# A weight-splitting planner that counts GpSimd and VectorE as excluding each other on SBUF operands

## The chip, the cores and the metric

The kernel runs on one core of a Trainium2 chip. The metric is the device time of one execution in microseconds (us). A core has five engines with a queue each: TensorE (PE in the rows; PEld is its weight load), VectorE (DVE), ScalarE (ACT), GpSimd (POOL) and SyncE (SP), which here issues all DMAs. Each engine takes its instructions strictly in the order in which they were written, and waits on semaphores for the others.

## The reference, cut to what matters

One decoder block over x of 512 x 1024 in float32: an RMS norm, one wide projection, two token mixers (sparse attention with compressed, selected and sliding branches, and chunkwise retention with 4 heads), gates, an output projection and a residual.

```python
h = rms_norm(x, norm_pre)
proj = h @ w_in                                   # 1024 x 6936
o_a = nsa(q_n, k_c, v_c, k_s, v_s, k_w, v_w, g_n) # attention, 8 heads of 64
y_a = (o_a * silu(z_n)) @ w_nsa_o
o_b = retention(rope(q_r), rope(k_r), v_r)        # 4 heads, chunks of 128
y_b = (o_b * silu(z_r)) @ w_ret_o
merged = sigmoid(m_a) * y_a + sigmoid(m_b) * y_b
y = x + rms_norm(merged @ w_out, norm_post)
```

## The kernel before

Every large product is made of three matmuls on operands that were split into a high part (rounded to the matmul's fp32r type) and a low part (the rest): high times high, high times low, low times high. So each half of a loaded weight tile (`raw`, 128 x 1024, two halves of 128 x 512) needs two operations before TensorE can use it: a copy to `whi`, by `cp_any` (L167) on ScalarE or VectorE, and a subtraction `wlo = raw - whi`, by `split_lo` (L373) and `sub_split` on VectorE or GpSimd. There are 168 halves, 8 of them 280 columns wide (they go to `arena_r`), the rest 512. Nine pairs `whi`/`wlo` and three `raw` buffers stand ahead of TensorE.

The order of all instructions is made while the program is built, by a planner (class `Order`). Work is written as coroutines: `main` is the long row of weight matmuls (low priority), and tails (rotary embedding, softmax, retention chunks, gates) are spawned from it with higher priority. `Order` keeps a planned time for TensorE (`now`) and one for each other engine (`eng`); each helper adds its price in ns: `tt` for two-tensor operations (VectorE, or GpSimd with e="pool"), `ts`, `stt`, `cp_any`, `mm` for matmuls. Before TensorE's next piece is written, `Order.run` asks which coroutine could go on by the planned time. A tail's transposes or matmuls are thus written between the main matmuls at the place where the planner thinks their operands ready; if they are late on the chip, TensorE waits there, with the main matmuls queued behind.

The engine of a half is chosen by planned times as well. For `wlo`, with `DVE_BIAS` of 900 in GpSimd's favour:

```python
e = "dve" if max(od.eng["dve"], r) + 1.04 * c < max(od.eng["pool"], r) + 2.25 * c - DVE_BIAS else "pool"
```

In the order of the program the stages are: norm, keys and values (`tail_a`, `tail_c`, with `rope16` at L176 and `doubled` at L523), queries (`tail_q`), compression, attention (`att_head` with L798 and L185, `att_block`), retention (`tail_qk`, `ret`), and the gated outputs. The names in the rows: `bank` is PSUM; `arena_f`, `arena_r`, `nat`, `raw`, `whi`, `wlo` lie in SBUF; L197 are matmuls, L201 transposes.

Of the kernel before, what the change touches and what calls it, by code (L numbers as in the profile page):

```python
# [18 lines left out]
P = 128  # L19
# [10 lines left out]
LAG, PE_LAG = 150.0, 110.0  # L30
MARGIN = 50.0
WAKE = 5, 2
HOOKS = 1, 3, 4, 5
DVE_BIAS = 900


class Order:
# [4 lines left out]
    def __init__(self):  # L42
        self.now = 0.0
        self.eng = {"act": 0.0, "dve": 0.0, "pool": 0.0, "dma": 0.0}
        self.ring = 500.0
        self.cos = []
        self.flags = set()

# [8 lines left out]
        self.now = max(self.now, r + LAG + PE_LAG) + cost  # L57
        return self.now + 47

    def op(self, e, cost, r=0.0):  # L60
        self.eng[e] = max(self.eng[e], r + LAG) + cost
        return self.eng[e]

    def dma(self, nbytes, r=0.0, n=1):
# [49 lines left out]
def block_kernel(ctx: ExitStack, tc, x, norm_pre, w_in, b_gate, pe_k, w1_k, w2_k,  # L114
# [27 lines left out]
    od = Order()  # L142


    def size(a):
        n = 1
        for k in a.shape[1:]:
            n *= k
        return n

    def far(a):
        return a.space == PSUM

    def act_ns(o, i, k=0):
        return 0.833 * size(o) + (51 if far(i) else 93) + 93 * k

    def copy_ns(o, i, k=0):
        return (1.042 if far(i) else 0.521) * size(o) + 69 + 61 * k

    def lazy(*vals):  # L160
        return sum(v is not None and not isinstance(v, (int, float)) for v in vals)

    def act(o, i, func=AF.Copy, r=0.0, **kw):
        S.activation(o, i, func, **kw)  # L164
        return od.op("act", act_ns(o, i, lazy(*kw.values())), r)

    def cp_any(o, i, r=0.0):  # L167

        cd = copy_ns(o, i)
        if max(od.eng["act"], r) + act_ns(o, i) <= max(od.eng["dve"], r) + cd:  # L170
            return act(o, i, r=r)
        V.tensor_copy(o, i)  # L172
        return od.op("dve", cd, r)

    def tt(o, a, b, op, r=0.0, e="dve"):
        (V if e == "dve" else G).tensor_tensor(o, a, b, op=op)  # L176
        if op == OP.pow:
            return od.op(e, 300 + 164 * size(o), r)
        return od.op(e, (1.042 * size(o) + 69) if e == "dve" else (2.25 * size(o) + 73), r)

    def ts(o, a, s1, s2, op0, op1=None, r=0.0):
        if op1 is None:
            V.tensor_scalar(o, a, s1, None, op0=op0)
        else:
            V.tensor_scalar(o, a, s1, s2, op0=op0, op1=op1)  # L185
        return od.op("dve", copy_ns(o, a, lazy(s1, s2)), r)

    def stt(o, a, s, b, op0, op1, r=0.0):
        V.scalar_tensor_tensor(o, a, s, b, op0=op0, op1=op1)  # L189
        return od.op("dve", 1.042 * size(o) + 69 + 61 * lazy(s), r)  # L190

    def recip(o, a, r=0.0):
        V.reciprocal(o, a)
# [1 line left out]

    def mm(ps, a, b, start, stop, r=0.0, cost=None):
        T.matmul(ps, a, b, start=start, stop=stop)  # L197
        return od.pe(cost or max(0.4167 * size(b) + 2.5, 107 if a.shape[-1] > 64 else 54), r)

    def tr(ps, a, idn, r=0.0):  # L200
        T.transpose(ps, a, idn)  # L201
# [2 lines left out]
    def mm3(ps, ah, al, bh, bl, first, last, r=0.0):  # L204
        mm(ps, ah, bh, first, False, r)
        mm(ps, ah, bl, False, False)
        return mm(ps, al, bh, False, last)

    def sub_split(lo, src, hi, r, e="dve"):
        return tt(lo, src, f(hi), OP.subtract, r, e)  # L210
# [124 lines left out]
    def load_next():  # L335
        i = len(raws)
        if i < len(loads):
            raw = rp.tile([P, 1024], FT, name="raw", tag="raw", bufs=NR)
            loads[i][0](raw)
            raws.append((raw, od.dma(P * loads[i][1] * 4, parts[2 * (i - NR) + 1][2] if i >= NR else 0.0, loads[i][2])))  # L340
            for fn in hook.get(i, ()):
                fn()
# [5 lines left out]
    def splitter():  # L348
        for i, (_, n, _, perm) in enumerate(loads):
            for k in range(2):  # L350
                p = 2 * i + k
                own = KD <= p < 2 * KD
                yield lambda: own or in_ring(p) < in_ring(len(done)) + NW
                while len(raws) <= i:
                    load_next()
                r = max(raws[i][1], done[-1] if done and not own else 0.0)
                yield r
                m = n // 2
                src = raws[i][0][:, k * m:(k + 1) * m]
                if own:  # L360
                    hi, lo = WC[p - KD]
                else:
                    hi = wp.tile([P, 512], FR, name="whi", tag="whi", bufs=NW)
                    lo = wp.tile([P, 512], FR, name="wlo", tag="wlo", bufs=NW)
                vh, vl = hi[:, :m], lo[:, :m]
                if perm:
                    src = src.rearrange("p (g j c) -> p g j c", g=2, j=4)
                    vh, vl = (v.rearrange("p (j g c) -> p g j c", g=2, j=4) for v in (vh, vl))
                e = cp_any(vh, src, r)
                od.spawn(split_lo(p, hi, lo, src, vh, vl, e), 0)  # L370
                yield

    def split_lo(p, hi, lo, src, vh, vl, r):  # L373
        yield r
        c = size(vl)
        e = "dve" if max(od.eng["dve"], r) + 1.04 * c < max(od.eng["pool"], r) + 2.25 * c - DVE_BIAS else "pool"
        r = sub_split(vl, src, vh, r, e)
        yield lambda: len(parts) == p
        parts.append((hi, lo, r))
        if p % 2 and len(raws) <= p // 2 + NR:  # L380
            load_next()
# [61 lines left out]
    def norm_tile(t):  # L443
        yield lambda: t in xarr
        xa = xt[t]
        ss = sp.tile([P, 2], FT, name="ss", tag="ss", bufs=4)
        for i, (c, ra) in enumerate(xarr[t]):
            yield ra
            ra = act(junk[:, c], xa[:, c], AF.Square, scale=1.0 / 32.0, accum_out=ss[:, i:i + 1], r=ra)
        yield ra  # L450
        rv = sp.tile([P, 1], FT, name="rv", tag="rv", bufs=4)
        if len(xarr[t]) == 2:
            ra = ts(rv, ss[:, 0:1], ss[:, 1:2], 1e-6, OP.add, OP.add, ra)
        else:
            ra = ts(rv, ss[:, 0:1], 1e-6, None, OP.add, r=ra)
        rs = sp.tile([P, 1], FT, name="rr", tag="rr", bufs=4)
        ra = tt(rs, rv, nhalf[:, 0:1], OP.pow, ra, "pool")
        yield ra
        for half in range(2):
            hc = slice(half * 512, half * 512 + 512)  # L460
            ra = stt(xa[:, hc], xa[:, hc], rs, npre[half], OP.mult, OP.mult, ra)
            od.spawn(norm_half(t, half, ra), 0)
        if t == NT - 1:
            for b in npre:
                PS.put(b, ra)
# [35 lines left out]
    def rope16(v, t, shape, r, e="dve"):  # L501

        n = int(np.prod(shape))
        pat = {1: "p (a c) -> p a c", 2: "p (a b c) -> p a b c"}[len(shape)]
        kw = dict(zip("ab", shape))
        t1, t2 = (at(41 + 0.5 * i, n * 16).rearrange(pat, **kw) for i in range(2))

        def bc(a):
            c = a.shape[-1]
            for _ in shape:  # L510
                a = a.unsqueeze(1)
            return a.broadcast_to([P, *shape, c])
        ix = (slice(None),) * (1 + len(shape))
        lo, hi, al = ix + (slice(0, 8),), ix + (slice(8, 16),), ix + (slice(0, 16),)
        tt(t1, v[al], bc(ropen[:, t, 0:16]), OP.mult, r, e)
        tt(t2[lo], v[hi], bc(ropen[:, t, 16:24]), OP.mult, r, e)
        tt(t2[hi], v[lo], bc(ropen[:, t, 24:32]), OP.mult, r, e)
        return tt(v[al], t1, t2, OP.add, 0.0, e)

    def doubled(kn, a, b, kd, r):  # L520

        n = (b - a) // 64
        V.tensor_copy(kd.rearrange("p (a r c) -> p a r c", a=n, r=2),  # L523
                      kn[:, a:b].rearrange("p (a c) -> p a c", c=64).unsqueeze(2).broadcast_to([P, n, 2, 64]))
        return od.op("dve", 0.6 * n * P + 70, r)

    def keysT(kd, off, br, t, r):
        ps = yield from PT.get()
# [68 lines left out]
    def tail_z(j, ps, e):  # L597
        yield e
        e = act(szn[:, j, :], ps, AF.Tanh, r=e, scale=0.5)
        yield e  # L600
        e = stt(szn[:, j, :], szn[:, j, :], 1.0, ps, OP.add, OP.mult, e)
        ACC.put(ps, e)
        od.flags.add(f"Z{j}")

    def gates():
        yield od.need("C0", "C1", "C2", "C3")
        e = act(gate, gate, AF.Tanh, scale=0.5)
        yield e
        ts(gate, gate, 0.25, 0.25, OP.mult, OP.add, e)
        od.flags.add("gate")  # L610
# [32 lines left out]
    def compress(i, ph, e):  # L643
# [20 lines left out]
        e = act(u, u, AF.Tanh, scale=0.7978845608028654, r=e)  # L664
        yield e
        e = stt(hx, u, 1.0, hx, OP.add, OP.mult, e)
        po = yield from PT.get()
        if i == 0:
# [691 lines left out]
```

## Time and profile before

| | |
|---|---|
| median of 3 runs | 565.32 us (565.24 to 566.01) |
| profiled execution | 565.26 us, of which the span is 563.5 us |
| TensorE busy | 533.2 us, 95% of the span |
| VectorE busy | 395.3 us, 70% |
| ScalarE busy | 227.1 us, 40% |
| GpSimd busy | 204.1 us, 36% |
| DMA | 53.1 MB, mean 94 GB/s |

The span is what the profiler saw of the instructions; 1.8 us of the execution lie around it. Busy times of engines overlap. Matmuls are pipelined, so that a record of 0.39 us stands for one every 0.225 us. Records on VectorE overlap their successor by some 0.08 us as well, so what an operation takes of the engine is the distance of two starts.

### The profile page before, as it was taken

What the parts mean: (1) busy time and instruction counts of PE and PEld (TensorE: products, weight loads), DVE (VectorE), ACT (ScalarE), POOL (GpSimd) and SP (SyncE); (2) the same over time, 40 slices, a digit from 0 to 9 for tenths busy, and PEclk for the clock granted to TensorE, in tenths of its full rate; (3) what the DMA queues carried; (4) which work ended last, traced back from release to release, by engine and by line L of the source; (5) the groups of instructions that cost most, each with busy time, mean ns of one, the idle gap of its engine ahead of it and who ended that gap; (6) DMA issues with size and microseconds to landing.
All of it is one profiled execution on the core that took longest, in us unless ns stands there. A gap on an engine that the chain in (4) does not pass through costs nothing.

```text
span 563.5 us, 7554 instructions
## 1 busy us (share of the span) xinstructions
PE 533.2 (95%) x2668; PEld 440.7 (78%) x2668; DVE 395.3 (70%) x803; ACT 227.1 (40%) x502; POOL 204.1 (36%) x195
## 2 busy tenths in 40 slices
PE   7969998979999989999999999899999999999995
PEld 5748886868888868878787788787888888887885
DVE  5989569998979999877786657755555342637353
ACT  4632456754547755645242435341212221103211
POOL 7643105850240432635215534333422251505220
PEclk9998999989999999999999999999999999999999
DMA  7633003650040130421314331317340440524023
GB/s 260 199 110 102 19 1 112 173 162 4 7 143 1 43 108 24 145 76 42 109 33 136 99 89 41 109 33 242 116 133 22 129 130 22 153 70 148 17 96 113
DMA packets 33672, 53.13 MB, mean 94 GB/s; under 512 B 4065, under 2 KB 14177, under 8 KB 33634
## 3 DMA queue, kind: packets, MB, share of 16 engines
q1 hardware_dynamic: 33634, 52.65, 31.0%
q8 instruction: 21, 0.34, 0.2%
q14 instruction: 17, 0.14, 0.1%
HBM read 50.54 MB, written 2.10 MB: 93 GB/s over the span
## 4 chain that ended last, share of the span: by engine, by line
PE 61%; DVE 27%; issue 5%; DMA 3%; POOL 2%; ACT 2%; DVEq 0%; POOLq 0%; SPq 0%; ACTq 0%
PE bank L197 57%; DVE arena_f L176 5%; DVE arena_r L176 4%; PE bank L201 4%; DVE wlo L176 4%; DVE arena_f L185 3%; DVE whi L172 3%; DMA raw<-in_w_in_dram 3%; DVE arena_f L798 2%; DVE arena_f L189 1%; DVE nat L176 1%; POOL wlo L176 1%; POOL nat L176 1%; ACT arena_r L164 0%; ACT whi L164 0%
## 5 line engine op out<-in xcount | busy, mean ns | idle before, releaser
L176 POOL TENSOR_TENSOR wlo<-raw,whi 128x512 fp32r<-128x512 f32 x103 | 144.3, 1414 | 213.1 <-PE bank L197 92.7
L197 PE MATMUL bank<-whi,hTh 128*128 128x512 f32 x256 | 104.8, 409 | 0.3 <-ACT hTh L164 0.3
L197 PE MATMUL bank<-whi,hTl 128*128 128x512 f32 x256 | 100.8, 394 | 1.0 <-DVE hTl L176 1.0
L197 PE MATMUL bank<-wlo,hTh 128*128 128x512 f32 x256 | 100.6, 393 | 0.7 <-POOL wlo L176 0.7
L164 ACT ACTIVATE whi<-raw 128x512 fp32r<-128x512 f32 x100 | 62.0, 629 | 60.0 <-PE bank L197 41.6
L164 ACT ACTIVATE arena_r<-bank 128x512 fp32r<-128x512 f32 (+2 forms) x88 | 50.0, 573 | 68.0 <-PE bank L201 61.8
L172 DVE CAST whi<-raw 128x512 fp32r<-128x512 f32 x60 | 44.6, 747 | 45.5 <-PE bank L197 38.2
L197 PE MATMUL bank<-arena_r 128*128 128x256 f32 (+2 forms) x328 | 72.9, 341 | 3.5 <-DVE arena_r L176 3.0
L176 DVE TENSOR_TENSOR arena_r<-bank,arena_r 128x512 fp32r<-128x512 f32 (+2 forms) x80 | 52.0, 658 | 27.1 <-ACT arena_r L164 26.5
L176 DVE TENSOR_TENSOR wlo<-raw,whi 128x512 fp32r<-128x512 f32 x57 | 61.3, 1084 | 4.3 <-ACT whi L164 2.5
L197 PE MATMUL bank<-hTh,whi 128*128 128x512 f32 x160 | 63.3, 396 | 0.9 <-DVE whi L172 0.9
L197 PE MATMUL bank<-hTh,wlo 128*128 128x512 f32 x160 | 62.7, 392 | 0.8 <-POOL wlo L176 0.6
L197 PE MATMUL bank<-hTl,whi 128*128 128x512 f32 x160 | 62.4, 390 | 0.0
L197 PEld LDWEIGHTS bank<-arena_r 128*128 128x128 f32 x328 | 51.1, 191 | 11.8 <-DVE arena_r L176 5.5
L197 PE MATMUL bank<-arena_r,whi 128*128 128x512 f32 x192 | 59.1, 389 | 0.0
L197 PEld LDWEIGHTS bank<-whi,hTl 128*128 128x128 f32 x256 | 48.3, 189 | 12.1 <-DVE hTl L176 1.4
L201 PE MATMUL bank<-ident,arena_f 128*128 128x128 f32 (+1 forms) x294 | 45.3, 279 | 11.7 <-DVE arena_f L523 4.8
L197 PEld LDWEIGHTS bank<-wlo,hTh 128*128 128x128 f32 x256 | 48.4, 189 | 9.2 <-POOL wlo L176 1.2
L197 PEld LDWEIGHTS bank<-whi,hTh 128*128 128x128 f32 x256 | 48.3, 189 | 8.6 <-ACT hTh L164 0.5
L201 PEld LDWEIGHTS bank<-ident,arena_f 128*128 128x128 f32 (+1 forms) x294 | 35.1, 141 | 23.9 <-DVE arena_f L176 6.2
L164 ACT ACTIVATE arena_f<-bank 128x512 f32<-128x512 f32 (+2 forms) x42 | 22.3, 530 | 75.8 <-PE bank L197 75.4
L197 PE MATMUL bank<-whi,arena_r 128*128 128x512 f32 (+1 forms) x176 | 49.0, 353 | 0.1
(116 smaller groups left out, 792.2 us busy)
## 6 DMA issues: line engine op xcount, KB each, us to landing
raw<-in_w_in_dram SPq DMA_DIRECT2D x44, 512.0 KB, 3.7
raw<-in_w_in_dram SPq DMA_DIRECT2D x16, 256.0 KB, 3.2
raw<-in_w_ret_o_dram SPq DMA_DIRECT2D x8, 512.0 KB, 4.9
raw<-in_w_out_dram SPq DMA_DIRECT2D x8, 512.0 KB, 3.8
arena_f<-in_x_dram SPq DMA_DIRECT2D x7, 512.0 KB, 5.8
raw<-in_cmp_w_k_dram SPq DMA_DIRECT2D x8, 256.0 KB, 3.7
arena_f<-in_rope_r_dram SPq DMA_DIRECT2D x8, 256.0 KB, 2.7
raw<-in_cmp_w_v_dram SPq DMA_DIRECT2D x8, 256.0 KB, 3.5
```

The source lines that it names most:

```text
L164: S.activation(o, i, func, **kw)
L172: V.tensor_copy(o, i)
L176: (V if e == "dve" else G).tensor_tensor(o, a, b, op=op)
L185: V.tensor_scalar(o, a, s1, s2, op0=op0, op1=op1)
L189: V.scalar_tensor_tensor(o, a, s, b, op0=op0, op1=op1)
L197: T.matmul(ps, a, b, start=start, stop=stop)
L201: T.transpose(ps, a, idn)
L798: V.tensor_tensor_reduce(pv[:, b, :], sv[:, b, :], maskp[:, 512 - L:512], 1.0, -NEG, OP.add, OP.min, nm[:, b:b + 1])
```

## The change

The planner gets a second time, `port`. Operations on VectorE whose operands all lie in SBUF, and all on GpSimd, begin no earlier than `port` and move it to their end; `begin` gives the planned start. `split_lo` compares planned ends with `begin` for both engines, and its bias of 900 in GpSimd's favour is gone; `cp_any` gets a bias of 400 ns in ScalarE's favour. Some prices move: a GpSimd subtraction of 512 columns from 1225 to 1285 ns, a matmul of 512 columns from 216 to 228 ns, and the doubling copy. No arithmetic changes.

```diff
--- before.py
+++ after.py
@@ -31,7 +31,7 @@
 MARGIN = 50.0
 WAKE = 5, 2
 HOOKS = 1, 3, 4, 5
-DVE_BIAS = 900
+DVE_BIAS = 400
 
 
 class Order:
@@ -43,6 +43,7 @@
         self.now = 0.0
         self.eng = {"act": 0.0, "dve": 0.0, "pool": 0.0, "dma": 0.0}
         self.ring = 500.0
+        self.port = 0.0
         self.cos = []
         self.flags = set()
 
@@ -57,8 +58,14 @@
         self.now = max(self.now, r + LAG + PE_LAG) + cost
         return self.now + 47
 
-    def op(self, e, cost, r=0.0):
-        self.eng[e] = max(self.eng[e], r + LAG) + cost
+    def begin(self, e, r=0.0, port=False):
+        return max(self.eng[e], r + LAG, self.port if port else 0.0)
+
+    def op(self, e, cost, r=0.0, port=False):
+
+        self.eng[e] = self.begin(e, r, port) + cost
+        if port:
+            self.port = self.eng[e]
         return self.eng[e]
 
     def dma(self, nbytes, r=0.0, n=1):
@@ -151,6 +158,9 @@
     def far(a):
         return a.space == PSUM
 
+    def near(*aps):
+        return not any(far(a) for a in aps)
+
     def act_ns(o, i, k=0):
         return 0.833 * size(o) + (51 if far(i) else 93) + 93 * k
 
@@ -167,27 +177,27 @@
     def cp_any(o, i, r=0.0):
 
         cd = copy_ns(o, i)
-        if max(od.eng["act"], r) + act_ns(o, i) <= max(od.eng["dve"], r) + cd:
+        if od.begin("act", r) + act_ns(o, i) <= od.begin("dve", r, near(i)) + cd + DVE_BIAS:
             return act(o, i, r=r)
         V.tensor_copy(o, i)
-        return od.op("dve", cd, r)
+        return od.op("dve", cd, r, near(i))
 
     def tt(o, a, b, op, r=0.0, e="dve"):
         (V if e == "dve" else G).tensor_tensor(o, a, b, op=op)
         if op == OP.pow:
-            return od.op(e, 300 + 164 * size(o), r)
-        return od.op(e, (1.042 * size(o) + 69) if e == "dve" else (2.25 * size(o) + 73), r)
+            return od.op(e, 300 + 164 * size(o), r, True)
+        return od.op(e, (1.042 * size(o) + 69) if e == "dve" else (2.36 * size(o) + 77), r, e == "pool" or near(o, a, b))
 
     def ts(o, a, s1, s2, op0, op1=None, r=0.0):
         if op1 is None:
             V.tensor_scalar(o, a, s1, None, op0=op0)
         else:
             V.tensor_scalar(o, a, s1, s2, op0=op0, op1=op1)
-        return od.op("dve", copy_ns(o, a, lazy(s1, s2)), r)
+        return od.op("dve", copy_ns(o, a, lazy(s1, s2)), r, near(o, a))
 
     def stt(o, a, s, b, op0, op1, r=0.0):
         V.scalar_tensor_tensor(o, a, s, b, op0=op0, op1=op1)
-        return od.op("dve", 1.042 * size(o) + 69 + 61 * lazy(s), r)
+        return od.op("dve", 1.042 * size(o) + 69 + 61 * lazy(s), r, near(o, a, b))
 
     def recip(o, a, r=0.0):
         V.reciprocal(o, a)
@@ -195,7 +205,7 @@
 
     def mm(ps, a, b, start, stop, r=0.0, cost=None):
         T.matmul(ps, a, b, start=start, stop=stop)
-        return od.pe(cost or max(0.4167 * size(b) + 2.5, 107 if a.shape[-1] > 64 else 54), r)
+        return od.pe(cost or max(0.4435 * size(b) + 1, 107 if a.shape[-1] > 64 else 54), r)
 
     def tr(ps, a, idn, r=0.0):
         T.transpose(ps, a, idn)
@@ -373,7 +383,7 @@
     def split_lo(p, hi, lo, src, vh, vl, r):
         yield r
         c = size(vl)
-        e = "dve" if max(od.eng["dve"], r) + 1.04 * c < max(od.eng["pool"], r) + 2.25 * c - DVE_BIAS else "pool"
+        e = "dve" if od.begin("dve", r, True) + 1.04 * c < od.begin("pool", r, True) + 2.36 * c else "pool"
         r = sub_split(vl, src, vh, r, e)
         yield lambda: len(parts) == p
         parts.append((hi, lo, r))
@@ -522,7 +532,7 @@
         n = (b - a) // 64
         V.tensor_copy(kd.rearrange("p (a r c) -> p a r c", a=n, r=2),
                       kn[:, a:b].rearrange("p (a c) -> p a c", c=64).unsqueeze(2).broadcast_to([P, n, 2, 64]))
-        return od.op("dve", 0.6 * n * P + 70, r)
+        return od.op("dve", 0.53 * n * P + 70, r, True)
 
     def keysT(kd, off, br, t, r):
         ps = yield from PT.get()
```

All of the order of the program is made anew with this. Over the whole program the `wlo` operations of 512 columns go from 103 on GpSimd and 57 on VectorE to 11 and 149; the `whi` copies of 512 columns go from 100 on ScalarE and 60 on VectorE to 148 and 12; of the 280-column halves, 3 subtractions move from GpSimd to VectorE and 3 copies from VectorE to ScalarE. TensorE has the same matmuls in another interleaving. SyncE has the same DMAs; one load of `raw` stands one place earlier against its neighbours, and one pair later.

First place: VectorE in the stage of keys and values, around the rotary embedding of the third tile (`nat_104`), whose doubled keys (the COPY) are what TensorE transposes next. Before:

```order
L176 TENSOR_TENSOR arena_f<-bank_85,pe_113 64x2x7x16
L176 TENSOR_TENSOR arena_f<-nat_104,ropen 128x64
L176 TENSOR_TENSOR arena_f<-nat_104,ropen 128x4x8 x2
L176 TENSOR_TENSOR nat_104<-arena_f 128x2x2x16
L523 COPY arena_f<-nat_104 128x768
L176 TENSOR_TENSOR arena_f<-bank_86,pe_112 64x2x8x16 x2
L176 TENSOR_TENSOR arena_f<-bank_86,pe_113 64x2x8x16 x2
L176 TENSOR_TENSOR wlo<-raw,whi 128x512
L176 TENSOR_TENSOR arena_r<-bank_85,arena_r 128x2x128
```

After:

```order
L186 TENSOR_TENSOR arena_f<-bank_86,pe_113 64x2x7x16
L186 TENSOR_TENSOR arena_f<-nat_104,ropen 128x64
L186 TENSOR_TENSOR arena_f<-nat_104,ropen 128x4x8 x2
L186 TENSOR_TENSOR nat_104<-arena_f 128x2x2x16
L533 COPY arena_f<-nat_104 128x768
L186 TENSOR_TENSOR wlo<-raw,whi 128x512 x5
L186 TENSOR_TENSOR arena_r<-bank_85,arena_r 128x2x128
L186 TENSOR_TENSOR arena_f<-bank_86,pe_112 64x2x8x16 x2
```

Five subtractions now stand behind the COPY and ahead of the low part of the transposed keys (`arena_r`), which stands some places earlier against the sums with `pe`.

GpSimd at the same place; the operations on `nat` are the low parts of values. Before:

```order
L176 TENSOR_TENSOR arena_r<-nat_103,arena_r 128x64 x2
L176 TENSOR_TENSOR wlo<-raw,whi 128x512
L176 TENSOR_TENSOR arena_r<-nat_104,arena_r 128x64 x2
L176 TENSOR_TENSOR wlo<-raw,whi 128x512 x4
L176 TENSOR_TENSOR arena_r<-nat_102,arena_r 128x64 x2
L176 TENSOR_TENSOR wlo<-raw,whi 128x512
L176 TENSOR_TENSOR gate<-nat_103,bg 128x24
```

After:

```order
L186 TENSOR_TENSOR arena_r<-raw,arena_r 128x280
L186 TENSOR_TENSOR arena_r<-nat_103,arena_r 128x64 x2
L186 TENSOR_TENSOR arena_r<-nat_104,arena_r 128x64 x2
L186 TENSOR_TENSOR arena_r<-nat_102,arena_r 128x64 x2
L186 TENSOR_TENSOR gate<-nat_103,bg 128x24
```

The six subtractions of 512 columns are gone from GpSimd here.

Second place: VectorE at the start of attention, behind the rotary embedding of the queries in `nat_103`; L798 and L185 belong to the softmax of one head, `arena_r<-bank` are low parts that TensorE needs. Before:

```order
L176 TENSOR_TENSOR nat_103<-arena_f 128x8x16
L176 TENSOR_TENSOR arena_r<-bank_85,arena_r 128x512
L798 ISA arena_f,stat<-bank_84,maskp 128x512
L798 ISA stat 128x1
L172 CAST whi<-raw 128x512
L193 RECIPROCAL stat<-stat 128x1
L185 TENSOR_SCALAR arena_f<-arena_f,stat,gate 128x512
L176 TENSOR_TENSOR arena_r<-nat_103,arena_r 128x8x64
L176 TENSOR_TENSOR arena_r<-bank_86,arena_r 128x512
```

After:

```order
L186 TENSOR_TENSOR arena_r<-nat_103,arena_r 128x8x64
L808 ISA arena_f,stat<-bank_84,maskp 128x512
L808 ISA stat 128x1
L186 TENSOR_TENSOR arena_r<-bank_85,arena_r 128x512
L182 CAST whi<-raw 128x512
L203 RECIPROCAL stat<-stat 128x1
L195 TENSOR_SCALAR arena_f<-arena_f,stat,gate 128x512
L186 TENSOR_TENSOR arena_r<-bank_86,arena_r 128x512
L186 TENSOR_TENSOR wlo<-raw,whi 128x512 x3
```

Three subtractions in a row stand on VectorE here now; before, four in a row of this stretch stood on GpSimd.

## Rows read from the trace of the kernel before

**Rows 1.** Windows: length, busy PE, PEld, DVE, ACT, POOL; clock, DMA share, GB/s.

```profile
0.00:60.00 60.00, 49.77 (x258) 39.16 (x259) 48.62 (x99) 25.57 (x61) 31.87 (x56) 0.97 0.51 157
60.00:130.00 70.00, 64.02 (x356) 53.28 (x355) 59.49 (x137) 41.91 (x93) 28.08 (x24) 0.98 0.33 95
130.00:260.00 130.00, 127.42 (x675) 106.12 (x674) 113.27 (x304) 73.23 (x188) 41.16 (x35) 1.00 0.20 59
260.00:400.00 140.00, 134.55 (x671) 111.36 (x670) 91.68 (x165) 52.48 (x97) 53.39 (x45) 1.00 0.32 96
...
400.00:563.50 163.50, 157.45 (x716) 130.81 (x714) 82.29 (x102) 33.95 (x64) 49.61 (x37) 1.00 0.31 97
```

**Rows 2.** Waits of TensorE: us in total, times, longest.

```profile
PE bank L197 <- DVE arena_r L176: 5.2, 6, 2.3
PE bank L201 <- DVE arena_f L523: 4.8, 2, 3.8
...
PE bank L201 <- DVE hTl L176: 1.3, 1, 1.3
```

**Rows 3.** Groups by line and shape: count, busy us, mean ns, idle before.

```profile
L176 POOL TENSOR_TENSOR wlo<-raw,whi 128x512 fp32r<-128x512 f32 x103 | 144.3, 1414 | 213.1 <-PE bank L197 92.7 <-DVE whi L172 44.9 <-ACT whi L164 34.8
...
L164 ACT ACTIVATE whi<-raw 128x512 fp32r<-128x512 f32 x100 | 62.0, 629 | 60.0 <-PE bank L197 41.6 <-DMA raw<-in_w_in_dram 12.4 <-DMA raw<-in_w_out_dram 3.1
L176 DVE TENSOR_TENSOR wlo<-raw,whi 128x512 fp32r<-128x512 f32 x57 | 61.3, 1084 | 4.3 <-ACT whi L164 2.5
...
L172 DVE CAST whi<-raw 128x512 fp32r<-128x512 f32 x60 | 44.6, 747 | 45.5 <-PE bank L197 38.2 <-DMA raw<-in_w_ret_o_dram 2.7 <-DMA raw<-in_w_in_dram 2.1
```

**Rows 4.** Timeline, VectorE where GpSimd is idle: start, us, operation, count.

```profile
14.88 0.69 DVE L176 TENSOR_TENSOR wlo<-raw,whi 128x512 fp32r<-128x512 f32 x1
15.49 0.42 DVE L172 CAST whi<-raw 128x512 fp32r<-128x512 f32 x1
15.83 0.68 DVE L176 TENSOR_TENSOR hTl<-bank,hTh 128x512 fp32r<-128x512 f32 x1
...
23.15 0.23 DVE L176 TENSOR_TENSOR nat<-arena_f 128x64 f32<-128x64 f32 x1
```

**Rows 5.** Timeline at the first place, 36 to 43 us, three engines.

```profile
36.34 4.98 POOL L176 TENSOR_TENSOR wlo<-raw,whi 128x512 fp32r<-128x512 f32 x4 [0.76 <-ACT whi L164]
...
36.95 3.19 DVE L176 TENSOR_TENSOR arena_f<-nat,ropen 128x64 f32<-128x64 f32 x3
40.18 1.22 DVE L176 TENSOR_TENSOR nat<-arena_f 128x64 f32<-128x64 f32 x1
...
42.05 0.44 PE L201 MATMUL bank<-ident,arena_f 128*128 128x128 f32 x2 [3.79 <-DVE arena_f L523]
```

**Rows 6.** Windows of a clock dip and of a dense stretch; columns as in rows 1.

```profile
43.30:46.70 3.40, 3.12 (x10) 2.15 (x9) 3.28 (x6) 0.00 (x0) 0.00 (x0) 0.50 0.12 34
...
450.00:500.00 50.00, 50.00 (x223) 41.39 (x222) 22.80 (x27) 9.23 (x15) 17.07 (x12) 1.00 0.36 106
```

**Rows 7.** Timeline of the second place and the longest wait of that stage.

```profile
86.95 5.84 POOL L176 TENSOR_TENSOR wlo<-raw,whi 128x512 fp32r<-128x512 f32 x4 [22.31 <-DVE stat L193]
...
86.92 1.61 DVE L185 TENSOR_SCALAR arena_f<-arena_f,stat,gate 128x512 f32<-128x512 f32 x1
88.45 1.78 DVE L176 TENSOR_TENSOR arena_r<-nat,arena_r 128x512 fp32r<-128x512 f32 x1
...
94.51 0.55 DVE L185 TENSOR_SCALAR arena_f<-arena_f,stat,gate 128x512 f32<-128x512 f32 x1
...
122.08 1.11 PE L197 MATMUL bank<-arena_f 128*128 128x64 f32 x4 [2.27 <-DVE arena_r L176]
```

**Rows 8.** Timeline in retention, 349 to 355 us.

```profile
349.41 3.00 POOL L176 TENSOR_TENSOR wlo<-raw,whi 128x512 fp32r<-128x512 f32 x2
...
351.18 1.78 DVE L176 TENSOR_TENSOR arena_r<-arena_f,arena_r 128x512 fp32r<-128x512 f32 x1
...
354.14 0.66 PE L201 MATMUL bank<-ident,arena_f 128*128 128x128 f32 x4 [1.15 <-DVE arena_f L176]
```

## Prediction, made before the changed kernel ran

> **What bounds the kernel now.** I read the windows by stage first [rows 1]. Their TensorE busy times add up to 533.2 of 563.5 us, so TensorE sets the end and what can be won is its idle time: 10.2 us from 0 to 60 (60 minus 49.8), 6.0 from 60 to 130, 2.6 from 130 to 260, 5.5 from 260 to 400 and 6.1 in the rest. From 450 to 500 us TensorE has no gap, at 50/222 = 0.225 us a matmul of 512 columns [rows 6]; what is idle behind 400 us is all but wholly the end of the last tail (norm, residual, store), and about 2 us at the beginning are start-up. So some 22 us of the idle time lie where an order can reach it. It is not lack of DMA: its share is 0.20 to 0.32 between 130 and 400 us [rows 1].
>
> The waits of TensorE come next [rows 2]: nearly all name VectorE. The groups and the timeline then say why VectorE is late. Its `wlo` takes 1084 ns in the mean and its copy to `whi` 747 [rows 3], but 0.69 and 0.42 us where GpSimd is idle [rows 4]. At the first place GpSimd runs four `wlo` from 36.34 to 41.32 us, and in that time VectorE spends 3.19 us on three tiny rotary products and 1.22 on a fourth operation [rows 5] that takes 0.23 alone [rows 4]: each waits out one GpSimd subtraction of about 1.25 us. The COPY behind them releases TensorE after 3.79 us idle. The planner before knows nothing of this, so it wrote the transposes where VectorE would have been ready without it. At the second place the same: 1.61 and 1.78 us for operations that take 0.55 and some 0.69 alone, beside four GpSimd subtractions [rows 4, 7]; and in retention 1.78 us instead of 0.69 ahead of a wait of 1.15 [rows 8].
>
> Idle time costs a second time: behind the waits of 3.79 and 2.27 us the granted clock is 0.50 (the level of 1.2 GHz) for 3.4 us, with 3.12 us busy [rows 5 to 7]. That is some 1.5 us of lost matmul time, at two places, of which [rows 6] show the first: 3 us in all.
>
> **The change part by part.**
>
> *92 subtractions of 512 columns go from GpSimd to VectorE, 48 copies from VectorE to ScalarE.* On VectorE a subtraction costs 0.61 us from start to start and a copy 0.34 [rows 4], so 92 x 0.61 - 48 x 0.34 = 56 - 16 = +40 us of work. Against it stands the time in which VectorE no longer waits for GpSimd. From below: the stretch of `wlo` and `whi` alone is 57 x (1.08 - 0.69) + 60 x (0.75 - 0.42) = 22 + 20 = 42 us [rows 3, 4], over 103 GpSimd subtractions 0.41 us each. From above: at the second place the two stretched operations beside four subtractions lost 1.06 + 1.09 = 2.15 us and a third, not in the rows, about as much, so 0.8 each. 92 x 0.41 to 92 x 0.8 is 38 to 74 us. VectorE's load therefore changes by +2 to -34 us of 395. I take -15: the many small operations of the first stage are in neither group of rows 3. VectorE gets little lighter, but its times get to be those that the planner reckons with, and that is the gain.
>
> ScalarE takes 48 x 0.63 = 30 us more [rows 3], on 227 busy; in its fullest stretch (130 to 260 us, 73 of 130) it gets some 6 more. This is covered; without that cover it would be late low parts, one copy of 0.63 each. GpSimd's own tails (rotary differences, low parts of values) no longer queue behind subtractions; I cost that at nothing. One weight load moves a place earlier on SyncE and a pair moves later; they lie tiles ahead in the ring of three `raw` buffers, so nothing, and one landing of some 4 us if that ring ran dry.
>
> *0 to 60 us.* The wait of 3.79 goes: four operations that cost 4.4 us [rows 5] cost about 0.65 without GpSimd's four subtractions, and the five that come to VectorE stand behind the COPY. Behind these five are the low part of the transposed keys and the sums with `pe`: 3.0 us later at worst, with the next transposes waiting for them, but the main matmuls have then been placed by a planner that counts these 3.0 us. The wait of 1.3 on `hTl` [rows 2] has the same rotary operations ahead of it and goes too. Of the 10.2 idle, 2 are start-up and 5.1 these two; of the 3.1 left I take half, and the clock dip of 1.5. Sum 3.8 + 1.3 + 1.5 + 1.5 = 8.1; bounds 3.8 and 9.6.
>
> *60 to 130 us.* VectorE is busy for 59.5 of 70 us and GpSimd for 28 [rows 1], nearly all with `wlo` (28/1.41 is 20). By the order 17 of these go to VectorE and 5 copies leave it: 17 x 0.61 - 5 x 0.34 = +8.7 us, against 17 x 0.41 to 0.8 = 7 to 14. So VectorE stays nearly as full as it is, and only the surprise goes. Of 6.0 idle and 1.5 of clock I take half, 3.7; bounds 0 and 7.5.
>
> *130 to 260 us.* 2.6 idle, VectorE 87% busy: I take 1.0; bounds -2 and 2.6.
>
> *260 to 400 us.* VectorE is 65% busy, and most of the 5.5 us are waits of 1.15 like that of [rows 8], behind two blocked operations. A blocked one loses about 1.1 us, the whole wait. I take 3.0; bounds 1 and 5.5. Behind 400 us: nothing to gain, and 82 busy of 163 leaves VectorE room for the 29 subtractions that come to it there.
>
> *The dearer matmul.* The planner had 216 ns, the trace has 225 [rows 6], now it has 228. Work planned behind k matmuls had k x 9 ns of unplanned cover, and now has none. A tail of some 16 matmuls (3.6 us) loses 0.15 us. TensorE waits at some 20 places for a fifth of a microsecond or longer (8 of them in the first two lines of [rows 2]). If each gets 0.15 longer, 2.9 us come back; bounds 0 (all have slack) and 8 (a wait on each of some 50 tails).
>
> Sum: 8.1 + 3.7 + 1.0 + 3.0 - 2.9 = 12.9 us. From the profiled execution of 565.26 us that is 552.4; the median of the runs is 0.06 above it, which changes nothing.
>
> **The rivals.**
>
> *All of it goes.* If the waits vanish once the planner's times are right, the upper bounds hold: 9.6 + 7.5 + 2.6 + 5.5 = 25, less 4 for the new prices, is 21: 544. For it: every longer wait seen has a blocked VectorE operation ahead of it. Against it: from 60 to 130 us VectorE stays about as full as it is.
>
> *VectorE takes over.* If the lower bounds of stretch hold, the first stage gains 5 and retention 3, the middle nothing, and the new price takes its 2.9: some 5 us, 560.
>
> *Slower: the low parts queue on VectorE.* From 60 to 260 us VectorE is busy for 172.8 of 200 us [rows 1]. By the order 33 subtractions come to it there and 12 copies leave: 33 x 0.61 - 12 x 0.34 = +16 us. Each subtraction has priority over attention in the planner, and ahead of the softmax of a head stand now three in a row, 1.8 us. If the GpSimd operations that remain (low parts of values, gates, rotary differences) block as much as the removed ones did, VectorE fills, and TensorE waits as the work on VectorE is late: 16 more, less 5 won elsewhere: 576. It decides where less than some 16 us of stretch fall away between 60 and 260 us, under 0.48 us for each of the 33. The Trainium skill (Perfetto Trace Analysis, Optimizing Scalar/DVE Operations) says that with VectorE saturated, handing work to ScalarE or even GpSimd may help, and adds that the shared read port may undo this for GpSimd. By its first half this rival holds; by its second the forecast. The first place, where four tiny operations took 4.4 us, is for the second half.
>
> *It doesn't do what it says.* If the exclusion is not symmetrical as the planner has it (VectorE's stretch were only its own queue), durations on VectorE stay at 1.08 and 0.75 and the order is merely another one: within a few us of 565, either side. The plain 0.69 and 0.42 of [rows 4] speak against it.
>
> **How the numbers follow.** The forecast of 552.4 (548 to 557, which the middle terms span) gets 0.52, all of it goes 0.13, VectorE takes over 0.16, the slower rival 0.12, and an order that is merely another 0.07, a third of it faster, a third slower and a third in between. A measurement of this kernel tells 0.2% (1.1 us) from no change. The slower rival may end with half its price and so lie within that bound in a quarter of its chance. So faster 0.52 + 0.13 + 0.16 + 0.02 = 0.83, the same 0.05, slower 0.12. The range runs from 543, which leaves out 0.03 below, to 563.5, which leaves out the slower rival and the like, 0.17.
>
> **What would show each step right or wrong.** In the profile of the changed kernel `wlo` on VectorE should have a mean near 0.7 us and `whi` on ScalarE 148 entries at 0.63; GpSimd's busy time falls to some 75 us (204 less 92 x 1.41). The wait for the COPY of the doubled keys should be under 1 us, and the clock should show 1.00 where the two dips were. Waits of TensorE in retention should halve. I am wrong if VectorE's busy time rises above 400 us, if TensorE waits from 60 to 130 us for more than 6 us, or if new waits of `wlo` on VectorE show up among those of TensorE.

## The result, and the profile after

The changed kernel takes 551.18 us in the median of 4 runs (550.76 to 552.06), against 565.28 for the kernel before (564.8 to 566.01): a ratio of 0.9752, 95% interval 0.9735 to 0.9769. The forecast was 552.4.

The same windows as in [rows 1], of the changed kernel (length, busy PE, PEld, DVE, ACT, POOL; clock, DMA share, GB/s). They are cut by time, so each holds a little more of the program than its counterpart of before.

```profile
0.00:60.00 60.00, 55.80 (x301) 45.57 (x302) 47.42 (x113) 33.52 (x79) 17.42 (x45) 1.00 0.52 162
60.00:130.00 70.00, 67.36 (x379) 55.54 (x377) 58.66 (x158) 44.56 (x99) 1.30 (x1) 1.00 0.32 91
130.00:260.00 130.00, 125.02 (x636) 103.07 (x637) 112.33 (x306) 76.96 (x194) 26.95 (x25) 0.97 0.21 63
260.00:400.00 140.00, 140.00 (x702) 118.07 (x701) 86.75 (x171) 56.14 (x104) 23.94 (x25) 1.00 0.36 108
400.00:549.50 149.50, 143.66 (x657) 119.76 (x655) 63.44 (x102) 41.35 (x78) 2.18 (x4) 0.99 0.29 92
```

TensorE's idle time falls from 30.3 us (563.5 less 533.2) to 17.7 (549.5 less 531.8). From 0 to 60 us it goes from 10.2 to 4.2, from 60 to 130 from 6.0 to 2.6, and in retention and what follows, 260 to 400 us, from 5.5 to nothing. From 130 to 260 us, in attention, it rises from 2.6 to 5.0, and there a clock dip has appeared. GpSimd does next to nothing from 60 to 130 us, where it was busy for 28.

The groups of the splits after, as in [rows 3] (count, busy us, mean ns, idle before):

```profile
L186 DVE TENSOR_TENSOR wlo<-raw,whi 128x512 fp32r<-128x512 f32 x149 | 102.9, 722 | 49.1 <-ACT whi L174 47.8 <-PE bank L207 0.9
...
L174 ACT ACTIVATE whi<-raw 128x512 fp32r<-128x512 f32 x148 | 89.6, 627 | 57.9 <-PE bank L207 22.7 <-DMA raw<-in_w_in_dram 19.0 <-DMA raw<-in_w_nsa_o_dram 4.6
...
L186 POOL TENSOR_TENSOR wlo<-raw,whi 128x512 fp32r<-128x512 f32 x11 | 15.0, 1368 | 118.4 <-ACT whi L174 68.2 <-DVE arena_f L199 49.1 <-DVE whi L182 1.1
...
L182 DVE CAST whi<-raw 128x512 fp32r<-128x512 f32 x12 | 5.0, 425 | 7.1 <-PE bank L207 1.8 <-DMA raw<-in_w_in_dram 1.7 <-DMA raw<-in_w_out_dram 1.3
```

A subtraction on VectorE takes 722 ns where it took 1084, a copy 425 where it took 747, each within 40 ns of the undisturbed operations in [rows 4]. The page's first part says what this comes to: VectorE busy 368.6 us (395.3 before), ScalarE 252.5 (227.1), GpSimd 71.8 (204.1).

```profile
PE 531.8 (97%) x2668; PEld 442.0 (80%) x2668; DVE 368.6 (67%) x847; ACT 252.5 (46%) x553; POOL 71.8 (13%) x100
```

The first place, where [rows 5] showed four operations in 4.4 us. Timeline after (start, us, operation):

```profile
33.40 0.60 POOL L186 TENSOR_TENSOR arena_r<-nat,arena_r 128x64 fp32r<-128x64 f32 x2 [6.10 <-ACT arena_r L174]
...
31.31 5.01 DVE L186 TENSOR_TENSOR arena_f<-bank,pe 64x256 f32<-64x256 f32 x8 [1.06 <-PE bank L211]
36.33 0.43 DVE L186 TENSOR_TENSOR arena_f<-nat,ropen 128x64 f32<-128x64 f32 x3
36.79 0.23 DVE L186 TENSOR_TENSOR nat<-arena_f 128x64 f32<-128x64 f32 x1
37.05 0.56 DVE L533 COPY arena_f<-nat 128x768 f32<-128x768 f32 x1
37.53 1.89 DVE L186 TENSOR_TENSOR wlo<-raw,whi 128x512 fp32r<-128x512 f32 x3
...
37.67 0.44 PE L211 MATMUL bank<-ident,arena_f 128*128 128x128 f32 x2 [1.19 <-DVE arena_f L533]
```

The same four operations now take 0.7 us, the subtractions follow the COPY on VectorE, and TensorE waits 1.19 us instead of 3.79. What VectorE works on ahead of the rotary products are now eight sums with `pe`, 5.01 us without a gap; GpSimd's last operation there ended at 34.00.

What got worse shows most between 222 and 232 us. Timeline, and a window of the dip (columns as above):

```profile
222.54 1.37 POOL L186 TENSOR_TENSOR wlo<-raw,whi 128x512 fp32r<-128x512 f32 x1 [6.46 <-ACT whi L174]
...
223.43 0.64 PE L211 MATMUL bank<-ident,arena_f 128*96 128x128 f32 x4 [1.36 <-DVE arena_r L186]
...
225.43 0.80 PE L207 MATMUL bank<-arena_r 128*128 128x256 f32 x2 [1.35 <-DVE stat L808]
```

```profile
225.40:232.30 6.90, 6.65 (x21) 5.38 (x22) 6.57 (x28) 3.60 (x15) 3.12 (x3) 0.51 0.35 132
```

Two waits of 1.4 us two microseconds apart, behind a VectorE that is busy for 5.33 of the 5.4 us ahead of 225.4, and then a granted clock at the 1.2 GHz level for 6.8 us, where the kernel before had 3.4 us at each of two places (the first is in [rows 6]). GpSimd's subtractions are not what TensorE waits for here: in e12 below, which has the same order and none of them at this place, the two waits are 1.35 and 1.20 us and the clock is low for some 3.4 us.

This is new among the waits of TensorE (us in total, times, longest):

```profile
PE bank L207 <- DVE wlo L186: 1.5, 5, 0.5
```

In the kernel before, TensorE waited once, for 0.2 us, for a `wlo` of VectorE.

### The profile page after: what moved, and what is told of

It is laid out like the page before. It is cut to its first block, busy times and chain, and to the rows that moved or that the text cites. A ratio compares the mean times of both kernels' runs of the same rounds, so it can differ in the third digit from the quotient of the medians.

```text
span 549.5 us, 7510 instructions
## 1 busy us (share of the span) xinstructions
PE 531.8 (97%) x2668; PEld 442.0 (80%) x2668; DVE 368.6 (67%) x847; ACT 252.5 (46%) x553; POOL 71.8 (13%) x100
## 4 chain that ended last, share of the span: by engine, by line
PE 79%; DVE 14%; issue 3%; DMA 2%; ACT 1%; POOL 0%; SPq 0%; DVEq 0%; POOLq 0%; ACTq 0%
PE bank L207 74%; PE bank L211 5%; DVE wlo L186 3%; DVE arena_f L186 2%; DVE arena_r L186 2%; DVE arena_f L808 2%; DVE arena_f L195 1%; DMA raw<-in_cmp_w_v_dram 1%; DVE arena_f L199 1%; DMA raw<-in_w_in_dram 1%; DVE nat L186 0%; ACT arena_r L174 0%; DVE stat L203 0%; POOL wlo L186 0%; SPq L295 0%
## 5 line engine op out<-in xcount | busy, mean ns | idle before, releaser
L186 DVE TENSOR_TENSOR wlo<-raw,whi 128x512 fp32r<-128x512 f32 x149 | 102.9, 722 | 49.1 <-ACT whi L174 47.8
L174 ACT ACTIVATE whi<-raw 128x512 fp32r<-128x512 f32 x148 | 89.6, 627 | 57.9 <-PE bank L207 22.7
L207 PE MATMUL bank<-arena_r 128*128 128x256 f32 (+2 forms) x328 | 71.5, 340 | 2.0 <-DVE stat L808 1.6
L207 PEld LDWEIGHTS bank<-arena_r,whi 128*128 128x128 f32 x192 | 36.0, 188 | 7.5
L174 ACT ACTIVATE arena_f<-arena_f,stat 128x512 f32<-128x512 f32 (+3 forms) x64 | 35.3, 554 | 9.4 <-DVE stat L808 9.3
```

## The experiments

In all of them the arithmetic is unchanged. "Fixed order" means: the planner is run as in the named kernel, so the order in which all instructions are written is that kernel's, but the weight copies and subtractions are issued on engines taken from a list. So order and engines can be crossed. Ratios are to the kernel before on the same chip, with 95% intervals.

**Order against engines.** The edit of e1, in the changed kernel, cut to the two lines that name the engine (e2 is the same in the kernel before, with the other kernel's lists):

```diff
-                e = cp_any(vh, src, r)
+                e = cp_any(vh, src, r, HI_ON[p])     # planned as ever, issued on HI_ON
-        r = sub_split(vl, src, vh, r, e)
+        r = sub_split(vl, src, vh, r, e, {"d": "dve", "p": "pool"}[LO_ON[p]])
```

> The order of every engine's other work, and TensorE's, is that of the changed kernel; only the 168 copies and 168 subtractions are issued on the engines that the kernel before chose (103 subtractions of 512 columns on GpSimd, 60 copies on VectorE). Theory A (the gain is VectorE no longer waiting out GpSimd's subtractions): the stretched operations come back, wlo on VectorE near 1.0 us in the mean, TensorE idle 25 to 40 us, time 562 to 572 us. Rival B (the gain is the new interleaving of TensorE's work, whoever splits): 551 to 555 us.

> The mirror: the order of the kernel before, copies and subtractions issued on the engines of the changed kernel (11 subtractions on GpSimd, 12 copies on VectorE). Theory A: most of the gain without any new plan, wlo on VectorE near 0.72 us, the wait of 3.79 us at the doubled keys below 1, time 551 to 558 us. Rival B: 562 to 568 us. Rival C (what was taken from GpSimd fills VectorE): VectorE over 400 us busy and slower than 566 us.

| | engines as before | engines as after |
|---|---|---|
| order of before | 565.3 us | e2: 552.7, 0.9766 (0.9724 to 0.9808) |
| order of after | e1: 566.8, 1.0008 (0.9984 to 1.0033) | 551.2, 0.9752 (0.9735 to 0.9769) |

The engines carry all of the gain in either order; the order, with all that the planner now knows, carries none that these runs can tell.

In e2 the wait for the first place's COPY is gone, but not all of what e2 was expected to do came true. Five subtractions (3.1 us) now stand on VectorE ahead of the next COPY, where one stood, and TensorE waits 2.53 us there (0.98 before):

```profile
38.96 3.10 DVE L182 TENSOR_TENSOR wlo<-raw,whi 128x512 fp32r<-128x512 f32 x5
...
46.33 0.69 PE L207 MATMUL bank<-ident,arena_f 128*128 128x128 f32 x2 [2.53 <-DVE arena_f L529]
```

The groups and the page's first part of e1:

```profile
L192 DVE TENSOR_TENSOR wlo<-raw,whi 128x512 fp32r<-128x512 f32 x57 | 63.6, 1126 | 2.4 <-ACT whi L183 1.2
...
L185 DVE CAST whi<-raw 128x512 fp32r<-128x512 f32 x60 | 43.3, 726 | 43.3 <-PE bank L213 37.2 <-DMA raw<-in_w_nsa_o_dram 1.8 <-DMA raw<-in_w_ret_o_dram 1.4
```

```profile
PE 535.0 (95%) x2668; PEld 442.9 (78%) x2668; DVE 394.5 (70%) x803; ACT 226.4 (40%) x502; POOL 202.9 (36%) x195
```

With the subtractions back on GpSimd the stretch is back (1126 and 726 ns), and with it TensorE's idle time, 29.8 us. The timeline of e1 at the first place shows the mechanism again, in another order: GpSimd's four subtractions from 36.30 us, three tiny products in 2.74 us, TensorE idle for 3.55.

```profile
36.30 5.00 POOL L192 TENSOR_TENSOR wlo<-raw,whi 128x512 fp32r<-128x512 f32 x4
...
38.60 2.74 DVE L192 TENSOR_TENSOR arena_f<-nat,ropen 128x64 f32<-128x64 f32 x3
...
42.25 0.44 PE L217 MATMUL bank<-ident,arena_f 128*128 128x128 f32 x2 [3.55 <-DVE arena_f L539]
```

**Knowledge without other engines.** The changed planner, its prices and its `port`, but the engine of every half planned and issued as before (cut to the lines that choose):

```diff
-        if od.begin("act", r) + act_ns(o, i) <= od.begin("dve", r, near(i)) + cd + DVE_BIAS:
+        if on == "a":                                # HI_ON of the kernel before
-        e = "dve" if od.begin("dve", r, True) + 1.04 * c < od.begin("pool", r, True) + 2.36 * c else "pool"
+        e = "dve" if LO_ON[p] == "d" else "pool"
```

> The changed planner with its knowledge of the exclusion and its prices, but the engine of every half is fixed to the choice of the kernel before, and planned as such. Theory A: VectorE is stretched as before (busy 385 to 400 us), but the waits are planned around: 555 to 562 us, between the two kernels. Rival B (the knowledge does it all): 550 to 553 us.

570.4 us, 1.0073 (1.0049 to 1.0097): slower than the kernel before. Neither side expected that. The idle time of TensorE is 30.1 us, as before, only elsewhere: it waits 8.9 us for low parts in `arena_r` and 7.2 for `wlo` itself. The span is 4.1 us longer, and all of that is busy time: 537.5 us (533.2 before), at a mean granted clock of 0.984 (0.993). Knowing when VectorE will be blocked did not let the planner fill the time. But e3 also has the dearer matmul, which alone makes the kernel before 7.6 us slower (e4 below), and no run has the knowledge at the old price with the old engines.

```profile
PE bank L209 <- DVE arena_r L188: 8.9, 2, 4.5
PE bank L209 <- DVE wlo L188: 5.2, 5, 1.8
PE bank L209 <- POOL wlo L188: 2.0, 2, 1.3
```

**Which of the two moves.** In the order of before, e5 takes only the list of the subtractions from the changed kernel, e6 only that of the copies. Against e2 each puts one list back (lists cut to their first letters; a is ScalarE, d VectorE, p GpSimd):

```diff
-HI_ON = "adaaaa..."    # copies as after
+HI_ON = "daadad..."    # e5: copies as before
-LO_ON = "dpddpd..."    # subtractions as after
+LO_ON = "ppdppp..."    # e6: subtractions as before
```

> The order of the kernel before; only the subtractions are issued on the engines of the changed kernel (92 more of 512 columns on VectorE), the 60 copies stay on VectorE. Theory A (GpSimd's subtractions are the cause): wlo near 0.72 and whi near 0.43 us on VectorE, 553 to 557 us, at least two thirds of the 13 us. Rival (the copies to ScalarE carry much of it, since VectorE is too full with both): 558 to 564 us.

> The order of the kernel before; only the copies are issued on the engines of the changed kernel (48 more on ScalarE), GpSimd keeps its 103 subtractions. VectorE loses 48 copies of 0.75 us, some 36 us of its busy time. If a lighter VectorE is what counts: 555 to 560 us. If the exclusion is what counts (theory A): TensorE's waits behind blocked operations stay, 561 to 566 us.

e5 takes 559.0 us, 0.9891 (0.9856 to 0.9926), 6 us less than before; e6 takes 556.4, 0.9849 (0.9813 to 0.9885), 9 us less. Both together (e2) give 13. This is not what theory A said: the copies alone, with all of GpSimd's subtractions in place, are worth about as much as the subtractions alone (the two intervals overlap). The page's first part of e5 and then of e6:

```profile
PE 533.2 (96%) x2668; PEld 441.5 (79%) x2668; DVE 387.8 (70%) x898; ACT 226.7 (41%) x502; POOL 70.4 (13%) x100
```

```profile
PE 534.1 (96%) x2668; PEld 444.1 (80%) x2668; DVE 361.5 (65%) x752; ACT 253.8 (46%) x553; POOL 204.1 (37%) x195
```

VectorE's busy time falls by 7.5 us in e5 and by 33.8 in e6. In e5 that is 92 subtractions more and all its stretch less (719 ns and 464 in the mean). In e6, 48 of the copies at some 0.75 us are gone, some 0.33 us of each being stretch, while subtractions on VectorE are stretched more than ever (1215 ns). TensorE's idle time says where each helps: e5 loses 3.9 us of it from 260 to 400 us and 2.0 from 0 to 60, e6 loses 3.6 from 0 to 60 us, 2.1 from 130 to 260, and some 1.5 each from 60 to 130 and from 260 to 400. The largest of these, e5 and then e6 (compare [rows 1]):

```profile
260.00:400.00 140.00, 138.43 (x690) 115.12 (x689) 93.69 (x187) 53.00 (x99) 25.25 (x27) 1.00 0.34 103
...
0.00:60.00 60.00, 53.38 (x275) 42.83 (x276) 43.15 (x91) 31.01 (x73) 31.96 (x56) 0.94 0.52 157
```

The wait at the first place shows how different the two are. It belongs to the subtractions; e6 has it in full, and e5 does not have it at this COPY, but 2.81 us at the next, like e2:

```profile
35.74 3.73 POOL L182 TENSOR_TENSOR wlo<-raw,whi 128x512 fp32r<-128x512 f32 x3
...
35.79 2.51 DVE L182 TENSOR_TENSOR arena_f<-nat,ropen 128x32 f32<-128x32 f32 x2
38.33 1.22 DVE L182 TENSOR_TENSOR nat<-arena_f 128x64 f32<-128x64 f32 x1
...
40.20 0.69 PE L207 MATMUL bank<-ident,arena_f 128*128 128x128 f32 x2 [3.77 <-DVE arena_f L529]
```

So there are two contributions: VectorE is no longer held up at places where TensorE waits for it, and the copies leave VectorE. That the second acts through VectorE's load is how I read it, and is not shown: a copy on ScalarE also no longer stands in VectorE's queue between other work, and part of what it took there was stretch. Per microsecond of VectorE's busy time the first is worth more (6.2 us for 7.5, against 8.8 for 33.8).

**One line in the old planner.** e8 gives every subtraction to VectorE in the kernel before, planned so:

```diff
-        e = "dve" if max(od.eng["dve"], r) + 1.04 * c < max(od.eng["pool"], r) + 2.25 * c - DVE_BIAS else "pool"
+        e = "dve"
```

> The kernel before with one edit: every subtraction of a weight half goes to VectorE, planned so; no knowledge of the exclusion, old prices, old choice for the copies. Theory A: 549 to 556 us, the model of the exclusion buys little once GpSimd has no weight work. Rival (the model is needed for the GpSimd work that remains): 557 to 563 us.

556.9 us, 0.9866 (0.9820 to 0.9913): about half of the gain for one line (by the interval, from a third to three quarters), and between the two ranges that were expected. That the old planner still left 32 copies on VectorE, at 493 ns, is one known difference to the changed kernel (12).

**The price of a matmul.** e4 puts the price of 228 ns into the kernel before, e7 the old 216 into the changed one:

```diff
-        return od.pe(cost or max(0.4167 * size(b) + 2.5, 107 if a.shape[-1] > 64 else 54), r)
+        return od.pe(cost or max(0.4435 * size(b) + 1, 107 if a.shape[-1] > 64 else 54), r)
```

> The kernel before with one edit: the planner's price of a matmul of 512 columns 228 instead of 216 ns. The prediction's term (cover lost, 2.9 us of waits come back): 566 to 569 us. Rival (the better price is itself part of the gain): 558 to 564 us.

> The changed kernel with the planner's matmul price back at 216 ns for 512 columns. The prediction's term (the low price is cover for tails): 545 to 550 us, 2 to 6 less than the changed kernel. Rival (with the exclusion planned, the true price is the better one): 551 to 555 us.

e4: 573.6 us, 1.0135 (1.0096 to 1.0174), 7.6 us slower. e7: 560.2, 0.9913 (0.9883 to 0.9943), 9.0 slower than the changed kernel. The higher price costs in one kernel and the lower one in the other, so neither "cover" nor "the true price" explains both, and both runs lie outside the ranges of both theories. The next two runs moved each price by 1.5 ns only, to 229.6 in the changed kernel (e9) and to 217.4 in the one before (e10); each makes the order anew:

> The changed kernel with the planner's price of a 512-column matmul at 229.6 instead of 228.1 ns, 1.5 ns off, which makes the order anew. If the price acts smoothly, 550 to 553 us. If every new order is a draw (the 9 us of the old price in e7 were the reordering, not the price), anything from 550 to 560 us, and then terms of 3 us for a price mean nothing.

> The same on the kernel before: 217.4 instead of 215.9 ns. Smooth: 565 to 567 us, an eighth of the 7.6 us that 228 cost in e4. A draw: anything from 560 to 574 us.

e9 takes 549.0 us, 0.9697 (0.9655 to 0.9739), and e10 561.8, 0.9922 (0.9895 to 0.9949): 2 and 4 us better than the kernels they come from; e9 is even a little under both ranges expected of it. In the kernel before, 216, 217.4 and 228 ns give 565.7, 561.8 and 573.6 us, up and down; in the changed one 216, 228 and 229.6 give 560.2, 551.2 and 549.0, so there a real effect of the price is not excluded. Each new order also moves a few halves to other engines (e10 has 54 copies on VectorE, not 60). TensorE's busy and idle time and the granted clock tell what moved. The page's first part of e9, and of e4:

```profile
PE 529.6 (97%) x2668; PEld 439.4 (80%) x2668; DVE 368.4 (67%) x842; ACT 254.3 (47%) x555; POOL 74.9 (14%) x103
```

```profile
PE 538.2 (94%) x2668; PEld 445.5 (78%) x2668; DVE 391.6 (68%) x800; ACT 230.5 (40%) x504; POOL 202.8 (35%) x196
```

The same 2668 matmuls take 529.6 us of busy time in e9, whose span has a mean granted clock of 0.999, and 538.2 in e4, at 0.982; the idle time is 17.1 and 34.8. Against the kernel it comes from, e9's span has 2.2 us less busy and 0.6 less idle time, e4's 5.0 more and 4.5 more, e10's 0.4 less and 4.2 less. e9's trace has no dip of the clock while TensorE works, e4's has four, the kernel before two. So clock dips are part of what an order costs, and they differ from order to order. They differ between runs of one order too: 16 runs of the kernel before on one chip had mean clocks from 0.985 to 0.996 and took 563.55 to 569.4 us. e9 is the fastest kernel of this study; its interval lies below that of the changed kernel in part only (0.9655 to 0.9739 against 0.9735 to 0.9769).

**No choice at all, and the last eleven.** e11 gives all copies to ScalarE and all subtractions to VectorE, and plans so; e12 keeps the changed kernel's order and issues its last subtractions on VectorE.

```diff
-        if od.begin("act", r) + act_ns(o, i) <= od.begin("dve", r, near(i)) + cd + DVE_BIAS:
+        if True:                                     # e11
-        e = "dve" if od.begin("dve", r, True) + 1.04 * c < od.begin("pool", r, True) + 2.36 * c else "pool"
+        e = "dve"                                    # e11; e12 does it by a list, in the order as it is
```

> The changed planner without any choice: every copy of a weight half on ScalarE, every subtraction on VectorE, both planned so. If the engines are the whole gain and the choice by planned ends adds nothing: 548 to 554 us. If the halves that the planner still gives to GpSimd and VectorE matter: 554 to 560 us.

> The order of the changed kernel to the last instruction, with the remaining 11 subtractions of 512 columns and 3 of 280 issued on VectorE instead of GpSimd; the copies stay. Theory A: the last blocked operations go, 0.4 to 0.8 us less stretch each against 0.6 more work, so 549 to 552 us. If VectorE's load is what counts: 552 to 556 us.

e11: 553.0 us, 0.9776 (0.9723 to 0.9830). e12: 552.2, 0.9752 (0.9714 to 0.9790). Neither can be told from the changed kernel. e12 lies at the edge between its two ranges and decides nothing. So the choice by planned ends, which is what the change brings, has no gain over fixed engines that these runs can tell.

## Why the prediction was right, and where its working was not

**What bounds the kernel, and why VectorE was late.** Right as far as it goes: TensorE waited for VectorE, and GpSimd's subtractions stretched VectorE's operations. e1 and e2 show the engines to be the cause: with GpSimd's subtractions and the copies back, in either order, 565 to 567 us; without them 551 to 553. But the stretch that the prediction named as the reason is only some 6 us of it alone (e5), and some 5 on top of the copies (0.9766 of e2 against 0.9849 of e6).

**VectorE's load.** Taken as -15 us, between +2 and -34; it was -26.7. GpSimd was to fall to some 75 us and fell to 71.8; `wlo` was to have a mean near 0.7 and has 0.722. But what the load is worth was mis-stated. The sum credited only the surprise, and of the copies it said merely that ScalarE's idle time covers them. e6 shows that the copies alone are worth 9 us. That step failed: taking 34 us from VectorE, which is busy for 173 of 200 us in the middle stages, was itself a gain, although the rest was still blocked.

**The stages.** From 0 to 60 us I had 8.1: TensorE's idle time fell by 6.0, and the dip went (clock 0.97 to 1.00, some 1.5 us), 7.5 together; the wait for the COPY stayed at 1.19 and not under 1. From 60 to 130 us I had 3.7: 3.4 idle and the other dip, 4.9. From 260 to 400 us I had 3.0: it was all 5.5, the upper bound; e5 wins 3.9 of it in the old order, by the subtractions alone. From 130 to 260 us I had +1.0 with a lower bound of -2: idle time rose by 2.4, and 6.8 us at half the clock (6.65 of them busy) cost some 3.3 more, -5.7 in all, outside the bounds. The bound left out that a dip can come as well as go. This is one execution: the four runs had mean clocks from 0.991 to 0.996, and their times do not follow them (551.23 us at 0.991, 550.76 and 552.06 at 0.996). The four stages add up to 12.2; the span fell by 14.0, of which 12.6 are idle time and 1.4 busy time. The windows are cut by time and not by work, so only the totals are exact.

**The dearer matmul.** I took 2.9 us as coming back, between 0 and 8 (the 0.225 us of a matmul divide 50 us by 222; the 223 matmuls of [rows 6] give 0.224). The runs do not support the term. The same edit costs 7.6 us in one kernel and its reversal 9.0 in the other (e4, e7), and shifts of 1.5 ns gave 2 and 4 us (e9, e10). With the sign of it open, the sum of 12.9 stands nearer to the measured 14.1 than its parts deserve, and that is partly luck: it is too low in retention, too high in attention, holds a term that isn't one, and gives nothing for the copies.

**The rivals.** The slower one is refuted: VectorE's busy time fell, and between 60 and 260 us it is 171 of 200 us (172.8 before), with 33 more subtractions. Against its 16 us of added work some 18 us of stretch fell away (172.8 + 16 - 171), just above the 16 at which it put the border. "VectorE takes over" is half right: attention did not gain. "It doesn't do what it says" is refuted for the chip and half right for the planner: durations did fall to the undisturbed ones, but what the planner learned gains nothing by itself (e1, e3). Of the signs of being wrong, one came true in small: the new waits for `wlo` on VectorE, 1.5 us in all against 12.6 us of idle time won. By the Trainium skill (Perfetto Trace Analysis, Optimizing Scalar/DVE Operations), work may go from a saturated VectorE to ScalarE or GpSimd, the latter perhaps in vain for the shared port. Both halves are borne out here: the copies to ScalarE gave 9 us (e6), and taking the subtractions back from GpSimd gave 6 (e5).

What stays open: which of its reorderings bring the clock dips that make the planner with full knowledge and the old engines slower (e3), and whether the copies help by VectorE's load or by their place in its queue (e6). No run separates the first from a mere redraw of the order, nor the two readings of the second.

## What to carry to other kernels

An engine that looks 36% busy can be the cause of another's lateness: compare an operation's mean with its duration where the other engine is idle, before handing it work. Cross order and engines (issue on a list, keep the order) before crediting a planner; here a better model showed no gain except by the engines it chose, fixed engines did as well (e11), and the one-line version had about half. Count what the work costs the engine it leaves: the copies that went to ScalarE, busy for 40% of the time, gave as much as ending GpSimd's blocking. Do not price a scheduler's constant from one new order: shift it by a per cent first and see how far a redraw alone moves the time.

## What was not expected of the hardware

The exclusion is felt most by the smallest operations: a rotary operation of 128 x 64 that takes 0.23 us alone [rows 4] takes 1.22 beside GpSimd's subtractions [rows 5]; a copy of 512 columns takes 1.51 instead of 0.42. Operations with an input in PSUM were spared: in e1, where the stretch is back, 64 subtractions from `bank` have a mean of 684 ns. The copy is from the kernel before, beside the four subtractions in [rows 7]; the group is from e1:

```profile
91.57 1.51 DVE L172 CAST whi<-raw 128x512 fp32r<-128x512 f32 x1
...
L192 DVE TENSOR_TENSOR arena_r<-bank,arena_r 128x512 fp32r<-128x512 f32 x64 | 43.0, 684 | 22.2 <-ACT arena_r L177 22.1
```

And a clock dip is not tied to one long wait: the 3.79 us of before and the 3.77 of e6, or two waits of 1.4 us close together in the changed kernel, all come with TensorE at the 1.2 GHz level, for 3.4 us in the first case and 6.8 in the other two; in e6 the first 1.8 of them lie in the wait itself.
